# Lo-part stores on GpSimd's queue, and a reordered head of the out-projection, in a two-layer RWKV-7 / sparse-attention trunk

## The chip, the core and the metric

The kernel runs on one core of a Trainium2 chip, in one launch. The time is the device time of one execution, in microseconds (us); a kernel's time is the median of its runs. A core has five engines with a queue each, worked off in order: TensorE (PE; its weight loads are shown apart as PEld), VectorE (DVE), ScalarE (ACT), GpSimd (POOL) and SyncE (SP), which here only issues DMAs. Engines wait for one another through semaphores.

## The reference

A residual stream of 16 learned meta tokens and 512 tokens, 1024 wide, goes through two layers. All is float32.

```
for i in range(2):                                   # layer
    h = h + 0.5 * swiglu(rms_norm(h, g[0]), w_in[i, 0], w_out[i, 0])      # 1024 -> 2 x 2816 -> 1024
    hn = rms_norm(h, g[1])
    if i == 0: h = h + rwkv7_time_mix(hn, ...)
    else:      h = h + dsa_attention(hn, ...)
    h = h + 0.5 * swiglu(rms_norm(h, g[2]), w_in[i, 1], w_out[i, 1])
return h[:, 16:]

def rwkv7_time_mix(h, mix, w_r, w_k, w_v, w_o, ..., g1, g2, ...):
    xx = shift_by_one_token(h) - h
    xr, xw, xk, xv, xa, xg = h + xx * mix[0..5]       # six mixed inputs
    r, k, v = xr @ w_r, xk @ w_k, xv @ w_v
    decay, a = low-rank functions of xw, xa
    g = sigmoid(xg @ g1) @ g2                         # the gate, rank 160
    y = recurrence over the tokens, 16 heads of 64
    return ((group_norm(y) * lnx_g + lnx_b + bonus) * g) @ w_o            # the out-projection
```

## The kernel before

Activations lie transposed: channels on the 128 partitions in eight tiles (`d` or `m`, 0 to 7), tokens along the free axis. The tokens are cut into two ranges, A (272, the meta tokens among them) and B (256), and each stage is done for one range at a time. Every float32 product is made of three TensorE passes: weights and activations are split in a rounded part `hi` and the rest `lo`, and `mm3` adds hi x hi, hi x lo and lo x hi. An input tile with its two parts is a "pair" (`p`, 14 buffers); `acc` are four PSUM banks for long sums, `bg` three for short ones, `ry` one.

Weights come from HBM as units of 128 x 1024 (512 KB), in the order of use. For each, SP loads `wraw` (4 buffers), ScalarE rounds it to `whi` and VectorE subtracts to get `wlo` (4 buffers each). `Weights.take` hands TensorE a block and sees to it that the units up to `ahead` (two further on) are split. A part of the `wlo` is kept: "save" and "keep" units are written to HBM (`lo`) by a DMA on SP's queue, behind the subtraction, and a later "again" unit reads it back in place of the subtraction. There are 32 such stores: 26 in about the first 200 us, six (units 4 to 9 of the out-projection's weights) in the out-projection of A.

The order of the work is that of the program text; generators are interleaved by hand (`joined`, `early`, counting steps) and by a planner that estimates times (`run`). In layer 0 the second half of the first FFN for B (`f00b`) is followed by `joined`: the out-projection of A, with the first steps of the projection of B (`proj`) inside it. Later the FFN `f01a` of A is followed by the out-projection of B.

The FFN ends with residuals: `finish(m)` adds the sum of tile `m` to `h` (VectorE), squares the result for the next norm (ScalarE) and adds the square to `ss` (VectorE). A `Lag` holds such small work back for some ticks, and `lag.flush()` issues what is left at the end.

`outproj` begins with `gate(m)`: five matmuls give the gate of tile `m` in a `bg` bank; VectorE multiplies it with the recurrence's output (`tb`, for A in two pieces, 256 and 16 wide), ScalarE rounds the product and VectorE subtracts, which makes the pair that the out-projection reads. Three gates go first; then, for `d` = 0 to 7, gate `d + 3` and the three products of tile `d` into three `acc` banks; then, for `m` = 3 to 7, eight products and the residual (`end`). The statistics of the next norm for B are asked for at a given step (`early(..., at=9)`), on TensorE four matmuls of `ones` with `ss` and `last`, and on VectorE a Newton iteration on `nst`.

`proj` begins with mixes: `mix(i, d)` makes one of the 6 x 8 mixed inputs: VectorE writes the normed tile (`ynat`), the token difference (`bu`) and the mixed tile (`tb`), ScalarE rounds, and VectorE subtracts (`p`) when the next mix has been issued. For B the first three of them are done within the out-projection of A, one each at the steps 27, 31 and 35 of its 51; the first weights, those of the key, then go over the eight inputs in four banks at a time.

Of the kernel before, what the change touches and what calls it, by code (L numbers as in the profile page):

```python
# [202 lines left out]
class Weights:  # L203


    def __init__(self, nc, pool, dram, wall, plan, raw_bufs, bufs, ahead):
        units, order = plan
        self.nc, self.pool, self.dram, self.wall = nc, pool, dram, wall
        self.units, self.kind, self.key = [units[u] for u, _, _ in order], [o[1] for o in order], [o[2] for o in order]
        self.raw_bufs, self.bufs, self.ahead = raw_bufs, bufs, ahead  # L210
        self.flat = [(i, p) for i, unit in enumerate(self.units) if self.kind[i] != "save" for p in unit]
        start = 128 * np.concatenate([[0], np.cumsum([unit_width(u) for u in units])])
        self.start = [start[u] for u, _, _ in order]
        self.pos = self.nraw = self.nhi = self.nlo = self.nback = 0
        self.raw, self.hi, self.lo, self.saved = {}, {}, {}, {}

    def load(self):

# [20 lines left out]
    def split(self, last):  # L239

        while self.nlo <= min(last, len(self.units) - 1):
            u = self.nlo
            self.round(u)
            self.back(u)
            r = self.raw.pop(u)
            w = r.shape[1]
            if self.kind[u] != "again":
                lo = self.pool.tile([128, 1024], F32R, name="wlo", bufs=self.bufs)
                self.nc.vector.tensor_sub(lo[:, :w], r, self.hi[u][:, :w].bitcast(F32))
                self.lo[u] = lo  # L250
            if self.kind[u] in ("save", "keep"):
                d = self.saved[self.key[u]] = self.dram.tile([128, 1024], F32, name=f"lo{self.key[u]}")
                self.nc.sync.dma_start(d, lo.bitcast(F32))
            self.nlo += 1

    def back(self, last):
# [14 lines left out]
    def take(self, piece):  # L271
        u, (p, at) = self.flat[self.pos]
        assert p == piece, (self.pos, p, piece)
        n = self.ahead + ("save" in self.kind[u + 1:u + 4])
        self.split(u + n)
        self.back(u + 3)
        if at >= 512:
            self.round(u + n + 1)
        self.pos += 1
        s = slice(at, at + piece[3] - piece[2])  # L280
        return self.hi[u][:, s], self.lo[u][:, s]
# [253 lines left out]
def trunk(ctx, tc, wall, plan, h0, vec, cstd, gqk, out, stop=None, gap=0.0, share=400.0, slack=200.0, fulls={}):  # L535
# [176 lines left out]


    def ffn(l, j, r, X, HID, nxt=None, done=None, groups=(0, 4), norm=None, xdone=None, tanh=False,
            part=None, side=False):


        win, wout = f"win{l}{j}", f"wout{l}{j}"
# [34 lines left out]
        for g in range(*groups):  # L753
# [74 lines left out]
            for m in range(3, DT):  # L828
# [7 lines left out]
                    if f == f0 + 1:  # L836
                        next(steps, None)
                lag.later(1, lambda m=m, p=p: finish(m, p, last))
        lag.flush()


    chains = []
# [105 lines left out]
    def proj(R, norm, pairs, core, ahead, park=None):  # L948
# [76 lines left out]
        if pad:  # L1025
            for t in (R.BKV[:, :, 8, 1:3, pad:], R.P[:, :, 8, 1 + pad:], R.a[:, :, n:288]):
                nc.gpsimd.memset(t, 0.0)
        for _ in range(4 if park else 3):
            mixes(1)
            yield  # L1030

# [453 lines left out]
        e = shi[32:64, 1, :n]  # L1485
        nc.vector.tensor_sub(e, R.sg[32:64, 1, :n], e.bitcast(F32))

    def outproj(R, pairs, nxt, last=None):

        r = R.r  # L1490
        n = R.n - R.pad
        shi, slo = (t for _, t in R.gates)
        xs, slot = {}, {}

        def gate(m):
            p = bbank()
# [9 lines left out]
                nc.vector.scalar_tensor_tensor(t[:, 256:n], y[:, 8, :R.pad], col(LNB + m), p[:, 256:n],  # L1506
                                               op0=OP.add, op1=OP.mult)
            slot[m] = pairs.take()
            xs[m] = [slot[m][1][:, j, :n] for j in range(2)]
            split(*xs[m], t[:, :n])  # L1510

        def end(m, p):
            residual(m, r, p[:, :n], 1.0)
            nxt.add(m, r)

        for m in range(3):
            gate(m)
            yield
        ps = [bank() for _ in range(3)]
        for d in range(DT):  # L1520
            if d + 3 < DT:
                gate(d + 3)
            if d + 3 == DT - 1:
                for t in R.gates:
                    pairs.give(t)
                if last:
                    last()
# [21 lines left out]
                norms[0].add(i // 4 - 4, B)  # L1549
            yield c  # L1550

    def ffn_stage(l, j, r, nxt, name, X=None, steps=None, other=None, xdone=None, HID=None, part=None):
        norm = norms[3 * l + 2 * j]
        if other:
            X = Rows(pairs, r)
# [12 lines left out]
            X.give()  # L1568
            return xdone if xdone else iter(())

        main = ffn(l, j, r, X, HID, nxt, norm=norm if other else None, xdone=free, part=part)
        run(early(first(main), norm, B, at=64, X=lambda: other, start=180, every=30) if other else main, name)
        HID.give()

# [4 lines left out]
    def joined():  # L1579

        main = proj(RB, norms[1], pairs, core, stepsA)
        for i, c in enumerate(early(outproj(RA, pairs, norms[2]), norms[1], B, at=9, apart=4)):
            if i in (27, 31, 35):
                assert B in norms[1].rstd
                next(main)
            yield c
        yield from early(main, norms[2], A, at=100, apart=16)

    mid, right = ExitStack(), ExitStack()
    pairs = Pairs(right.enter_context(tile_pool("pairs", side="right")), 14)  # L1590
    core = mid.enter_context(tile_pool("core"))
# [32 lines left out]
            yield c  # L1624

    run(prefix(proj(RA, norms[1], pairs, core, stepsB, HB)), "pA")
    ffn_stage(0, 0, B, norms[1], "f00b", XB, stepsB, xdone=gates(RA), HID=HB, part="rest")
    drain()
    core_work(RB, core, S)
    run(joined(), "pB")  # L1630
    ffn_stage(0, 1, A, norms[3], "f01a", XA, stepsA, xdone=gates(RB))
    drain()
    XS = {}
    xa = []
# [15 lines left out]
        for _ in steps:  # L1650
            pass

    run(early(first_x(outproj(RB, pairs, norms[2], after)), norms[3], A, at=9, apart=4))
    right.close()
    xq = xa[0]

# [458 lines left out]
```

## Time and profile before

| | before |
|---|---|
| time, median of 3 runs (lowest, highest) | 2252.68 us (2248.6, 2252.9) |
| the profiled execution: its own time, its span | 2253.37 us, 2251.6 us |
| mean granted TensorE clock | 0.996 |
| moved by DMA | 405.66 MB, mean 180 GB/s |
| time of a 512 KB load of `wraw` / store of `lo` / read of `lo`, issue to landing | 3.5 / 4.2 / 4.4 us |

The profile is one execution. Times are us from the span's start. In rows of the trace, an operation stands as engine, line, operation, output<-input, shape; "[0.50 <-ACT p L387]" says that the engine stood idle 0.50 us before it and that ScalarE's work on `p` ended that. In lists of waits, the numbers are the total, the number and the longest. Nearly every instruction has the line of one helper, so that the names of the tiles tell them apart.

### The profile page before, as it was taken

The page shows a single profiled execution, that of the slowest core. Times are in us where ns is not written, and L with a number is a line of the kernel's source. Part 1 is how long each engine was busy: PE and PEld are TensorE (multiplying, and loading weights), DVE is VectorE, ACT ScalarE, POOL GpSimd, SP SyncE. Part 2 cuts the span into 40 slices and gives each one's busy share as a digit, 9 for nine tenths or more (in the row PEclk, how much of TensorE's full clock was granted, in tenths as well). Part 3 has the DMA queues.
Part 4 walks back from the last instruction along what each step waited for, and adds up shares of the span by engine and source line. Part 5 has one row for each costly group of instructions (what it writes and reads, how often), then busy time and mean ns, then how long its engine had stood idle before and what let it go on. Part 6 is the DMA issues. An engine that isn't in the chain of part 4 may idle for free.

```text
span 2251.6 us, 49304 instructions
## 1 busy us (share of the span) xinstructions
PE 2209.3 (98%) x20028; PEld 2147.2 (95%) x20028; DVE 1643.9 (73%) x3281; ACT 1261.6 (56%) x2189; POOL 70.5 (3%) x122
## 2 busy tenths in 40 slices
PE   8999999999999999999999999999999999999999
PEld 8999999999899999999999999899998989989999
DVE  7777787846878883676656659887667988867665
ACT  6555784486478447654445445556545645555443
POOL 0000002011000110000000000000000000000000
PEclk9999999999999999999999999999999999999999
DMA  8788766622585562365555655553455543435654
GB/s 283 276 295 280 277 217 236 197 68 88 198 296 177 161 195 79 103 221 185 178 172 167 194 164 169 164 172 129 144 180 162 172 151 106 149 104 179 191 184 140
DMA packets 115188, 405.66 MB, mean 180 GB/s; under 512 B 12993, under 2 KB 17169, under 8 KB 114961
## 3 DMA queue, kind: packets, MB, share of 16 engines
q1 hardware_dynamic: 112592, 397.07, 53.0%
q0 software_dynamic: 2368, 5.44, 0.9%
q8 instruction: 157, 2.57, 0.5%
q14 instruction: 71, 0.57, 0.1%
HBM read 380.88 MB, written 21.05 MB: 179 GB/s over the span
## 4 chain that ended last, share of the span: by engine, by line
PE 82%; DVE 10%; ACT 4%; issue 2%; DMA 1%; SPq 0%; ACTq 0%; DVEq 0%
PE acc L387 70%; PE bg L387 9%; PE ry L387 4%; DVE wlo L387 3%; DMA wraw<-wall 1%; ACT whi L387 1%; DVE tb L387 1%; DVE ynat L387 1%; DVE p L387 1%; DVE rel L387 1%; DVE h L387 1%; DVE m L387 0%; ACT pr L387 0%; DVE AR L387 0%; ACT p L387 0%
## 5 line engine op out<-in xcount | busy, mean ns | idle before, releaser
L387 ACT ACTIVATE whi<-wraw 128x1024 fp32r<-128x1024 f32 (+2 forms) x674 | 705.6, 1052 | 412.0 <-PE acc L387 244.3
L387 DVE TENSOR_TENSOR wlo<-wraw,whi 128x1024 fp32r<-128x1024 f32 (+3 forms) x628 | 766.1, 1223 | 187.8 <-ACT whi L387 173.4
L387 PE MATMUL acc<-p,whi 128*128 128x272 f32 (+1 forms) x4112 | 790.0, 291 | 14.6 <-ACT whi L387 6.7
L387 PEld LDWEIGHTS acc<-p,whi 128*128 128x128 f32 x4112 | 644.9, 190 | 23.7 <-DVE p L387 7.2
L387 PE MATMUL acc<-p,wlo 128*128 128x272 f32 (+1 forms) x2056 | 590.4, 287 | 0.2 <-DVE wlo L387 0.2
L387 PEld LDWEIGHTS acc<-p,wlo 128*128 128x128 f32 x2056 | 389.8, 190 | 0.6 <-DVE wlo L387 0.6
L387 PE MATMUL acc<-xa_hi,whi 128*128 128x256 f32 (+1 forms) x1072 | 306.6, 286 | 0.0
L387 PE MATMUL acc<-xa_hi,wlo 128*128 128x256 f32 (+1 forms) x1072 | 304.3, 284 | 1.0 <-DVE wlo L387 1.0
L387 PE MATMUL acc<-xa_lo,whi 128*128 128x256 f32 (+1 forms) x1072 | 303.7, 283 | 0.0
L387 PE MATMUL acc<-hid_hi,whi 128*128 128x256 f32 (+1 forms) x880 | 253.0, 288 | 1.3 <-DVE ta L387 1.0
L387 PE MATMUL acc<-hid_lo,whi 128*128 128x256 f32 (+1 forms) x880 | 250.1, 284 | 4.3 <-DVE hid_lo L387 4.3
L387 PE MATMUL acc<-hid_hi,wlo 128*128 128x256 f32 (+1 forms) x880 | 249.9, 284 | 0.0
L387 PE MATMUL acc<-xb_hi,whi 128*128 128x256 f32 x744 | 211.3, 284 | 0.0
L387 PE MATMUL acc<-xb_hi,wlo 128*128 128x256 f32 x744 | 208.7, 280 | 0.0
L387 PE MATMUL acc<-xb_lo,whi 128*128 128x256 f32 x744 | 208.6, 280 | 0.0
L387 PEld LDWEIGHTS acc<-xa_hi,whi 128*128 128x128 f32 x1072 | 202.8, 189 | 1.6 <-issue 1.5
L387 PEld LDWEIGHTS acc<-xa_hi,wlo 128*128 128x128 f32 x1072 | 202.7, 189 | 1.4 <-DVE wlo L387 1.4
L387 PEld LDWEIGHTS acc<-xa_lo,whi 128*128 128x128 f32 x1072 | 203.0, 189 | 0.0
L387 PEld LDWEIGHTS acc<-hid_lo,whi 128*128 128x128 f32 x880 | 168.1, 191 | 5.2 <-DVE hid_lo L387 5.2
L387 PEld LDWEIGHTS acc<-hid_hi,whi 128*128 128x128 f32 x880 | 166.9, 190 | 3.9 <-issue 1.9
L387 DVE SCALAR_TENSOR_TENSOR h<-acc,h 128x256 f32<-128x256 f32 (+1 forms) x288 | 117.3, 425 | 71.5 <-PE acc L387 71.2
L387 PEld LDWEIGHTS acc<-hid_hi,wlo 128*128 128x128 f32 x880 | 167.2, 190 | 0.0
(309 smaller groups left out, 3156.9 us busy)
## 6 DMA issues: line engine op xcount, KB each, us to landing
wraw<-wall SPq DMA_DIRECT2D x659, 512.0 KB, 3.5
wlo<-lo SPq DMA_DIRECT2D x46, 512.0 KB, 4.4
lo<-wlo SPq DMA_DIRECT2D x32, 512.0 KB, 4.2
wraw<-wall SPq DMA_DIRECT2D x10, 438.0 KB, 3.3
out<-h SPq DMA_DIRECT2D x8, 256.0 KB, 2.3
h<-h SPq DMA_DIRECT2D x2, 512.0 KB, 8.1
L<-gm POOLq DMA_DIRECT2D x16, 64.0 KB, 2.4
ynat<-L POOLq DMA_DIRECT2D x2, 512.0 KB, 4.9
```

Of the source, the lines that this page charges most:

```text
L387: r = f(*args, **kw)
```

## The change

It has five parts. The stores of `lo` are issued by GpSimd in place of SP. `gate` no longer subtracts at once: it leaves the subtraction to the next gate (`lower`), so that VectorE does gate `m + 1`'s multiplication between. The FFN ahead of an out-projection does not flush its lag: the out-projection gets it as `tail`, and ticks or flushes it after each of its first three gates. While these gates are issued, `W.hold` keeps `take` from splitting units ahead. And in `joined` the statistics for B are asked for at step 5 in place of 9, and five mixes of B are done ahead, at the steps 19, 24, 29, 34 and 39.

```diff
@@ -213,6 +213,7 @@
         self.start = [start[u] for u, _, _ in order]
         self.pos = self.nraw = self.nhi = self.nlo = self.nback = 0
         self.raw, self.hi, self.lo, self.saved = {}, {}, {}, {}
+        self.hold = False
 
     def load(self):
 
@@ -250,7 +251,7 @@
                 self.lo[u] = lo
             if self.kind[u] in ("save", "keep"):
                 d = self.saved[self.key[u]] = self.dram.tile([128, 1024], F32, name=f"lo{self.key[u]}")
-                self.nc.sync.dma_start(d, lo.bitcast(F32))
+                self.nc.gpsimd.dma_start(d, lo.bitcast(F32))
             self.nlo += 1
 
     def back(self, last):
@@ -271,7 +272,7 @@
     def take(self, piece):
         u, (p, at) = self.flat[self.pos]
         assert p == piece, (self.pos, p, piece)
-        n = self.ahead + ("save" in self.kind[u + 1:u + 4])
+        n = 0 if self.hold else self.ahead + ("save" in self.kind[u + 1:u + 4])
         self.split(u + n)
         self.back(u + 3)
         if at >= 512:
@@ -712,7 +713,7 @@
 
 
     def ffn(l, j, r, X, HID, nxt=None, done=None, groups=(0, 4), norm=None, xdone=None, tanh=False,
-            part=None, side=False):
+            part=None, side=False, tail=None):
 
 
         win, wout = f"win{l}{j}", f"wout{l}{j}"
@@ -836,7 +837,10 @@
                     if f == f0 + 1:
                         next(steps, None)
                 lag.later(1, lambda m=m, p=p: finish(m, p, last))
-        lag.flush()
+        if tail is None:
+            lag.flush()
+        else:
+            tail.append(lag)
 
 
     chains = []
@@ -1025,7 +1029,7 @@
         if pad:
             for t in (R.BKV[:, :, 8, 1:3, pad:], R.P[:, :, 8, 1 + pad:], R.a[:, :, n:288]):
                 nc.gpsimd.memset(t, 0.0)
-        for _ in range(4 if park else 3):
+        for _ in range(4 if park else 5):
             mixes(1)
             yield
 
@@ -1485,12 +1489,12 @@
         e = shi[32:64, 1, :n]
         nc.vector.tensor_sub(e, R.sg[32:64, 1, :n], e.bitcast(F32))
 
-    def outproj(R, pairs, nxt, last=None):
+    def outproj(R, pairs, nxt, tail, last=None):
 
         r = R.r
         n = R.n - R.pad
         shi, slo = (t for _, t in R.gates)
-        xs, slot = {}, {}
+        xs, slot, late = {}, {}, []
 
         def gate(m):
             p = bbank()
@@ -1506,20 +1510,34 @@
                 nc.vector.scalar_tensor_tensor(t[:, 256:n], y[:, 8, :R.pad], col(LNB + m), p[:, 256:n],
                                                op0=OP.add, op1=OP.mult)
             slot[m] = pairs.take()
-            xs[m] = [slot[m][1][:, j, :n] for j in range(2)]
-            split(*xs[m], t[:, :n])
+            hi, lo = xs[m] = [slot[m][1][:, j, :n] for j in range(2)]
+            lower()
+            nc.scalar.activation(hi, t[:, :n], AF.Copy)
+            late.append(lambda: nc.vector.tensor_sub(lo, t[:, :n], hi.bitcast(F32)))
+
+        def lower():
+            while late:
+                late.pop()()
 
         def end(m, p):
             residual(m, r, p[:, :n], 1.0)
             nxt.add(m, r)
 
+        W.hold = True
         for m in range(3):
             gate(m)
+            if m < 2:
+                tail.tick()
+            else:
+                tail.flush()
             yield
+        W.hold = False
         ps = [bank() for _ in range(3)]
         for d in range(DT):
             if d + 3 < DT:
                 gate(d + 3)
+            else:
+                lower()
             if d + 3 == DT - 1:
                 for t in R.gates:
                     pairs.give(t)
@@ -1549,7 +1567,7 @@
                 norms[0].add(i // 4 - 4, B)
             yield c
 
-    def ffn_stage(l, j, r, nxt, name, X=None, steps=None, other=None, xdone=None, HID=None, part=None):
+    def ffn_stage(l, j, r, nxt, name, X=None, steps=None, other=None, xdone=None, HID=None, part=None, tail=None):
         norm = norms[3 * l + 2 * j]
         if other:
             X = Rows(pairs, r)
@@ -1568,7 +1586,8 @@
             X.give()
             return xdone if xdone else iter(())
 
-        main = ffn(l, j, r, X, HID, nxt, norm=norm if other else None, xdone=free, part=part)
+        main = ffn(l, j, r, X, HID, nxt, norm=norm if other else None, xdone=free, part=part,
+                   tail=tail)
         run(early(first(main), norm, B, at=64, X=lambda: other, start=180, every=30) if other else main, name)
         HID.give()
 
@@ -1579,13 +1598,14 @@
     def joined():
 
         main = proj(RB, norms[1], pairs, core, stepsA)
-        for i, c in enumerate(early(outproj(RA, pairs, norms[2]), norms[1], B, at=9, apart=4)):
-            if i in (27, 31, 35):
+        for i, c in enumerate(early(outproj(RA, pairs, norms[2], *tails[0]), norms[1], B, at=5, apart=4)):
+            if i in (19, 24, 29, 34, 39):
                 assert B in norms[1].rstd
                 next(main)
             yield c
         yield from early(main, norms[2], A, at=100, apart=16)
 
+    tails = [], []
     mid, right = ExitStack(), ExitStack()
     pairs = Pairs(right.enter_context(tile_pool("pairs", side="right")), 14)
     core = mid.enter_context(tile_pool("core"))
@@ -1624,11 +1644,11 @@
             yield c
 
     run(prefix(proj(RA, norms[1], pairs, core, stepsB, HB)), "pA")
-    ffn_stage(0, 0, B, norms[1], "f00b", XB, stepsB, xdone=gates(RA), HID=HB, part="rest")
+    ffn_stage(0, 0, B, norms[1], "f00b", XB, stepsB, xdone=gates(RA), HID=HB, part="rest", tail=tails[0])
     drain()
     core_work(RB, core, S)
     run(joined(), "pB")
-    ffn_stage(0, 1, A, norms[3], "f01a", XA, stepsA, xdone=gates(RB))
+    ffn_stage(0, 1, A, norms[3], "f01a", XA, stepsA, xdone=gates(RB), tail=tails[1])
     drain()
     XS = {}
     xa = []
@@ -1650,7 +1670,7 @@
         for _ in steps:
             pass
 
-    run(early(first_x(outproj(RB, pairs, norms[2], after)), norms[3], A, at=9, apart=4))
+    run(early(first_x(outproj(RB, pairs, norms[2], *tails[1], after)), norms[3], A, at=9, apart=4))
     right.close()
     xq = xa[0]
 
```

TensorE's queue keeps its order but for those statistics and the spreading of their result, which come earlier. VectorE's first gates of A, before: `h_71<-acc` are the FFN's residuals, `ss` sums of squares, `tb` and `p` a gate's product and its subtraction, `wlo` a weight subtraction.

```order
L387 SCALAR_TENSOR_TENSOR h_71<-acc_7961,h_71 128x256
L387 TENSOR_TENSOR ss_7901<-ss_7901,tb_7994 128x256
L387 SCALAR_TENSOR_TENSOR h_71<-acc_7982,h_71 128x256
L387 TENSOR_TENSOR ss_7901<-ss_7901,tb_8004 128x256
L387 TENSOR_TENSOR wlo_8011<-wraw_7834,whi_7985 128x1024
L387 SCALAR_TENSOR_TENSOR tb_8018<-AR_4001,vecs_83,bg_8010 128x256
L387 SCALAR_TENSOR_TENSOR tb_8018<-AR_4001,vecs_83,bg_8010 128x16
L387 TENSOR_TENSOR p2_8021<-tb_8018,p2_8021 128x272
L387 SCALAR_TENSOR_TENSOR tb_8030<-AR_4001,vecs_83,bg_8024 128x256
L387 SCALAR_TENSOR_TENSOR tb_8030<-AR_4001,vecs_83,bg_8024 128x16
L387 TENSOR_TENSOR p9_8033<-tb_8030,p9_8033 128x272
```

The same place of VectorE's queue now:

```order
L388 SCALAR_TENSOR_TENSOR h_71<-acc_7961,h_71 128x256
L388 SCALAR_TENSOR_TENSOR tb_8009<-AR_4001,vecs_83,bg_8003 128x256
L388 SCALAR_TENSOR_TENSOR tb_8009<-AR_4001,vecs_83,bg_8003 128x16
L388 TENSOR_TENSOR ss_7901<-ss_7901,tb_7994 128x256
L388 SCALAR_TENSOR_TENSOR h_71<-acc_7982,h_71 128x256
L388 SCALAR_TENSOR_TENSOR tb_8024<-AR_4001,vecs_83,bg_8018 128x256
L388 SCALAR_TENSOR_TENSOR tb_8024<-AR_4001,vecs_83,bg_8018 128x16
L388 TENSOR_TENSOR p2_8012<-tb_8009,p2_8012 128x272
L388 TENSOR_TENSOR ss_7901<-ss_7901,tb_8015 128x256
L388 SCALAR_TENSOR_TENSOR tb_8039<-AR_4001,vecs_83,bg_8033 128x256
L388 SCALAR_TENSOR_TENSOR tb_8039<-AR_4001,vecs_83,bg_8033 128x16
L388 TENSOR_TENSOR p9_8027<-tb_8024,p9_8027 128x272
```

The first product stands ahead of the last residual, the first weight subtraction (`wlo_8011` before) behind all of this, and a gate's subtraction behind the next gate's product.

VectorE's queue at the first mixes of B, before (residuals `h_71<-acc` are those of the out-projection of A; the residual in the first row is that of `m` = 5):

```order
L387 SCALAR_TENSOR_TENSOR h_71<-acc_8326,h_71 128x272
L387 TENSOR_TENSOR ss_8237<-ss_8237,tb_8385 128x272
L387 SCALAR_TENSOR_TENSOR ynat_8336<-h_71,vecs_83,rstd_8283 128x256
L387 TENSOR_TENSOR bu_8340<-ynat_8336 128x256
L387 SCALAR_TENSOR_TENSOR tb_8396<-bu_8340,vecs_83,ynat_8336 128x256
L387 TENSOR_TENSOR p3_8352<-tb_8350,p3_8352 128x256
L387 SCALAR_TENSOR_TENSOR h_71<-acc_8388,h_71 128x272
L387 TENSOR_TENSOR ss_8237<-ss_8237,tb_8427 128x272
L387 SCALAR_TENSOR_TENSOR h_71<-acc_8430,h_71 128x272
```

The same place of VectorE's queue now, from the fourth mix on:

```order
L388 TENSOR_TENSOR p7_8337<-tb_8335,p7_8337 128x256
L388 SCALAR_TENSOR_TENSOR h_71<-acc_8349,h_71 128x272
L388 TENSOR_TENSOR ss_8242<-ss_8242,tb_8399 128x272
L388 SCALAR_TENSOR_TENSOR ynat_8298<-h_71,vecs_83,rstd_8239 128x256
L388 TENSOR_TENSOR bu_8302<-ynat_8298 128x256
L388 SCALAR_TENSOR_TENSOR tb_8426<-bu_8302,vecs_83,ynat_8298 128x256
L388 TENSOR_TENSOR p0_8369<-tb_8367,p0_8369 128x256
L388 SCALAR_TENSOR_TENSOR h_71<-acc_8402,h_71 128x272
L388 TENSOR_TENSOR ss_8242<-ss_8242,tb_8441 128x272
L388 SCALAR_TENSOR_TENSOR h_71<-acc_8444,h_71 128x272
```

The last three residuals had two, three and three mixes ahead of them; now they have four, five and five, and three subtractions of mixes are done before the last two residuals in place of one.

GpSimd's queue in the out-projection of A, which held only the clears (`MEMSET`) there, now, with the six stores (`lo18` to `lo23`):

```order
L388 MEMSET p4_7907 128x272
L388 DMA lo18_8105<-wlo_8103 128x1024
L388 DMA lo19_8167<-wlo_8165 128x1024
L388 DMA lo20_8206<-wlo_8204 128x1024
L388 DMA lo21_8255<-wlo_8253 128x1024
L388 DMA lo22_8292<-wlo_8290 128x1024
L388 MEMSET gm_8304 128x64
L388 DMA lo23_8352<-wlo_8350 128x1024
L388 MEMSET rs_9294 128x288
```

The clear of `gm` (a column of B's decays) stands behind five stores, each of which waits for its subtraction; on SP's queue the loads follow one another without them.

## The prediction

> **What bounds the kernel now.** I read the page's busy shares first, then TensorE's waits over the stretch that the change touches, then that stretch engine by engine in order of time.
>
> ```profile
> PE 2209.3 (98%) x20028; PEld 2147.2 (95%) x20028; DVE 1643.9 (73%) x3281; ACT 1261.6 (56%) x2189; POOL 70.5 (3%) x122
> ```
>
> TensorE is busy 98% of 2251.6 us, so a change that leaves its matmuls alone can win only its pauses (some 42 us) and the time that it runs at a lower clock. Two lists of what TensorE waited for follow: 540 to 660 us, which holds the out-projection of the first token range (A), and 975 to 1030 us, which holds that of the second (B).
>
> ```profile
> PE acc L387 <- DVE p L387: 3.7, 3, 1.8
> PE bg L387 <- DVE tb L387: 1.8, 1, 1.8
> PE acc L387 <- DVE h L387: 0.4, 1, 0.4
> ...
> PE bg L387 <- DVE tb L387: 0.6, 1, 0.6
> ```
>
> All are waits for VectorE. At A they fall at 587.8 us (fourth gate), 621.4 us (first mixed input of the next projection) and shortly after; one of the 3.7 us stands earlier, in the FFN. The stage table (us, TensorE busy, weight loads, VectorE, ScalarE, POOL, clock, DMA) shows that they cost more than their length:
>
> ```profile
> 585.00:590.00 5.00, 3.18 (x20) 2.91 (x19) 3.87 (x11) 1.96 (x5) 0.00 (x0) 0.88 0.44 151
> 590.00:595.00 5.00, 5.00 (x33) 5.00 (x33) 3.65 (x10) 2.64 (x5) 0.00 (x0) 0.78 0.00 0
> ...
> 620.00:625.00 5.00, 2.67 (x13) 2.17 (x14) 4.30 (x12) 2.98 (x7) 0.00 (x0) 0.79 1.02 415
> 625.00:630.00 5.00, 5.00 (x25) 5.00 (x26) 4.79 (x13) 3.01 (x5) 0.00 (x0) 0.53 1.02 399
> ```
>
> After either pause the granted clock falls; the four rows lose 5 x (0.12 + 0.22 + 0.21 + 0.47) = 5.1 us to it.
>
> Under those pauses VectorE is never free for long. Its queue at the gates of A:
>
> ```profile
> 584.30 0.42 DVE L387 SCALAR_TENSOR_TENSOR h<-acc,h 128x256 f32<-128x256 f32 x1
> 584.64 0.41 DVE L387 TENSOR_TENSOR ss<-ss,tb 128x256 f32<-128x256 f32 x1
> ...
> 585.87 1.22 DVE L387 TENSOR_TENSOR wlo<-wraw,whi 128x1024 fp32r<-128x1024 f32 x1
> 587.00 0.62 DVE L387 SCALAR_TENSOR_TENSOR tb<-AR,vecs,bg 128x256 f32<-128x256 f32 x2
> 588.12 0.44 DVE L387 TENSOR_TENSOR p<-tb,p 128x272 fp32r<-128x272 f32 x1 [0.50 <-ACT p L387]
> 588.48 0.61 DVE L387 SCALAR_TENSOR_TENSOR tb<-AR,vecs,bg 128x256 f32<-128x256 f32 x2
> 589.59 0.44 DVE L387 TENSOR_TENSOR p<-tb,p 128x272 fp32r<-128x272 f32 x1 [0.50 <-ACT p L387]
> ...
> 601.83 0.44 DVE L387 TENSOR_TENSOR p<-tb,p 128x272 fp32r<-128x272 f32 x1 [0.50 <-ACT p L387]
> 602.78 1.23 DVE L387 TENSOR_TENSOR wlo<-wraw,whi 128x1024 fp32r<-128x1024 f32 x1 [0.51 <-ACT whi L387]
> 603.92 0.15 DVE L387 TENSOR_SCALAR nst<-bg 128x2 f32<-128x2 f32 x1
> ...
> 606.16 0.78 DVE L387 SCALAR_TENSOR_TENSOR h<-acc,h 128x272 f32<-128x272 f32 x2
> 607.50 0.44 DVE L387 TENSOR_TENSOR ss<-ss,tb 128x272 f32<-128x272 f32 x1 [0.56 <-ACT tb L387]
> ```
>
> Each of the eight gates makes VectorE stand 0.50 us for ScalarE's rounding before it can subtract. From start to start, a weight subtraction takes 1.13, a residual or a sum of squares 0.34, a gate's multiply pair with its subtraction 0.90 (1.47 less 0.50, and less the overlap of back-to-back work), the norm's statistics 2.24 (603.92 to 606.16). Then the mixes, two of TensorE's groups of three, and ScalarE's first copy of a finished key group:
>
> ```profile
> 620.95 0.41 DVE L387 TENSOR_TENSOR p<-tb,p 128x256 fp32r<-128x256 f32 x1
> 621.29 0.43 DVE L387 SCALAR_TENSOR_TENSOR h<-acc,h 128x272 f32<-128x272 f32 x1
> 622.27 0.44 DVE L387 TENSOR_TENSOR ss<-ss,tb 128x272 f32<-128x272 f32 x1 [0.56 <-ACT tb L387]
> ...
> 622.98 0.48 DVE L387 SCALAR_TENSOR_TENSOR ynat<-h,vecs,rstd 128x256 f32<-128x256 f32 x1
> ...
> 624.36 0.42 DVE L387 TENSOR_TENSOR p<-tb,p 128x256 fp32r<-128x256 f32 x1
> 624.69 0.48 DVE L387 SCALAR_TENSOR_TENSOR ynat<-h,vecs,rstd 128x256 f32<-128x256 f32 x1
> ...
> 630.20 0.40 PE L387 MATMUL acc<-p,whi 128*128 128x256 f32 x2
> ...
> 630.56 0.40 PE L387 MATMUL acc<-p,whi 128*128 128x256 f32 x2
> ...
> 631.20 0.42 DVE L387 TENSOR_TENSOR p<-tb,p 128x256 fp32r<-128x256 f32 x1
> ...
> 635.07 0.39 ACT L387 ACTIVATE BKV<-acc 128x256 f32<-128x256 f32 x1 [1.53 <-PE acc L387]
> ```
>
> A mix of the first kind with its subtraction costs 1.71 us (622.98 to 624.69); the eight inputs are served at that pace, the sixth at 631.20. TensorE needs 0.36 us for three matmuls, 1.43 for an input's twelve. So from 584 to 632 us the path is VectorE's queue, and a place in that queue is worth something only by the bubbles that it closes.
>
> **The change part by part.** *Gates in front of the last residuals, subtraction one gate late, weight work held.* No instruction is added. Laid end to end from 584.30 in the new order: two residuals and two sums 1.36, eight gates 7.2, five weight subtractions 5.65 (as many as before up to that point), the statistics 2.24, now between the fifth and sixth subtraction of a gate: 16.5, so A's first output residual comes at 600.8 instead of 606.16, 5.4 earlier. Of it 8 x 0.50 + 0.51 = 4.5 are named waits. The fourth gate's bank is free when its third has issued, so the 1.8 us pause goes. What is late next: at 0.125 a matmul a gate takes TensorE 0.62 and an input's nine 1.13, so it is ready for the sixth gate's input at 595.7, which now stands behind the statistics and comes at 597.1; a pause of some 1.4, and one of 0.8 at the seventh, which cost nothing as long as VectorE sets the end. The hold makes the third weight unit's subtraction 2 us later (587.9), read by TensorE at 589.7.
>
> *Five mixes from the 20th step instead of three from the 28th.* Same work, moved ahead of three of the residuals that follow. From 600.8 in the new order, a residual and its sum 1.3 (0.99 of it to the sum, with the 0.56 wait for ScalarE), weight work 1.13, mixes 1.38 to 1.71: the first input is ready at 614.6, before TensorE wants it (617: the last gate's matmuls end at 601.4, and the 120 that follow take 0.125 each), the third at 619.4, the sixth at 626.0 against 631.20. Late next: the key group needs four banks, and the third and fourth are given back by the last two residuals, now behind the fifth mix, at 619.9 and 621.2. TensorE then pauses about 3 us around 618 to 621, and then runs 1.43 us per input behind the mixes: the first key copy comes at 629.5 against 635.07. I take 5.6 us for A; bounds: 2.2, if two more stretches at half clock (6.8 us, a loss of 3.4) follow that pause, and 10.2 less B's 0.6, if every pause named (1.8 + 1.8 + 0.4 + 0.5 + 0.6 = 5.1) and all 5.1 us of low clock went. Nearest is VectorE's queue, which leads both ends.
>
> *The same gates at B* have 0.6 us to win; the first input's subtraction comes some 0.25 after TensorE could use it: 0.4 (0 to 0.6).
>
> *Stores by POOL.* 32 issues move from SP, 26 of them in the first 200 us, six at A.
>
> ```profile
> lo<-wlo SPq DMA_DIRECT2D x32, 512.0 KB, 4.2
> ynat<-L POOLq DMA_DIRECT2D x2, 512.0 KB, 4.9
> DVE wlo L387 <- DMA lo<-wlo: 11.6, 6, 2.6
> 20.00:200.00 180.00, 179.35 (x1430) 178.71 (x1430) 135.08 (x226) 96.15 (x135) 0.00 (x0) 1.00 0.80 278
> L387 POOL DMA_DIRECT2D L<-gm x18: 584/648/730, 367.3 to 779.5; - x18
> ```
>
> The loads behind a store on SP's queue wait for the same subtraction anyway, since it frees the raw buffer that they fill; what a load gains is the issue of 0.33 us and a shorter line. TensorE pauses 0.65 us in those 180 us, so at most 0.7 is to be won. Worst, each store lands 0.7 later (4.9 against 4.2) and all of it reaches TensorE: 32 x 0.7 = 22. But VectorE already stands 11.6 us behind store landings without a pause of TensorE, being two weight units ahead (24 matmuls each, at 179.35 / 1430 = 0.125: 6.0 us): I take 0. POOL pays 32 x 0.65 us; it is 97% idle, and what stands behind its stores at A, a clear of a decay column, is first read by the scan at 666:
>
> ```profile
> 666.20 0.71 DVE L387 TENSOR_TENSOR_SCAN gm<-reset,gm 128x264 f32<-128x264 f32 x1 [3.39 <-ACT gm L387]
> ```
>
> Sum: 5.6 + 0.4 + 0 = 6.0 off the profiled execution, 2253.4 to 2247.4. That execution was 0.7 above the median of the three runs shown, so against 2252.7 I predict 2246.7.
>
> *A rule beside a row.* The clock fell after a pause of 1.8 us with matmuls on both sides. The Trainium skill's page "TensorE: Matmul & The Clock Gate" (What's actually happening) lets the clock drop after at least one idle window of about 3.4 us. By that rule no pause here would cost clock, and removing all of them would give 5.1; the rows show the 5.1 of lost clock as well, and the rows decide.
>
> **The rivals.** *New pauses eat it.* For it: VectorE's queue is no shorter, and residuals now stand behind mixes. Gain 2.2 + 0.4 at the low bound, up to 4: 2248.7 to 2250.1. Against: the bubbles closed (4.5) are real waits in the rows.
>
> *All pauses and all low clock go.* 10.2 off: 2242.5. Against: the queue laid end to end closes only 5.4.
>
> *POOL's stores come too late: slower.* If a store issued by POOL starts much later than SP's did while VectorE is busy, the weight buffer stays taken, VectorE waits, then TensorE. It decides once a store lands over 6 us later than now; at 0.5 us reaching TensorE for each of 26 stores, 13 us: 2259.7. Against: POOL issued 18 transfers in 584 to 730 ns each in stretches where VectorE was busy. The Trainium skill's page "SBUF — State Buffer" (SBUF: two separate sides) says that VectorE's two-port modes lock GpSimd out of the port through which it writes its descriptors; those issues show none of it.
>
> **How the numbers follow.** My case, 4 to 7 us: 0.55; new pauses, 1 to 4: 0.25; everything goes: 0.13; slower: 0.07. Within 0.2% (4.5 us) is about what a measurement here cannot tell from no change. Faster by more: nine tenths of the first and the third, 0.63; same: the rest of the first and the second, 0.32; slower: 0.05, as some of that case stays within 0.2%. The range reaches from the third case's edge, 2243.5, to the weak end of the second, 2251.5.
>
> **What would show it.** Right: no 0.50 waits at A's gates, first residual near 601, first key copy near 629.5, a pause of TensorE for a residual near 619, no pause over 1 us at the fourth gate. Wrong: half clock still after 619 for two stretches, the first key copy after 632, or TensorE pausing for weights before 200 us.

## The result, and the profile after

The changed kernel takes 2269.78 us (median of 6 runs, 2267.28 to 2271.33) against 2251.55 (2248.6 to 2252.9) of the kernel before on the same chip: a ratio of 1.0084, with a 95% interval of 1.0073 to 1.0094. It is slower by 0.84%, 18 us. The profiled executions differ by less, 2267.28 against 2253.37, 13.9 us; the sums below are made against those.

From the page of the changed kernel, the busy shares and the stores of `lo` (size, median us from issue to landing):

```profile
PE 2208.7 (97%) x20028; PEld 2145.2 (95%) x20028; DVE 1642.4 (72%) x3281; ACT 1260.4 (56%) x2189; POOL 86.4 (4%) x154
...
lo<-wlo POOLq DMA_DIRECT2D x32, 512.0 KB, 6.3
```

A store now lands 6.3 us after its issue, where it was 4.2. The stage table of the changed kernel shows where that matters (columns as in the prediction), and the same first two stretches of before stand behind it:

```profile
20.00:98.00 78.00, 77.70 (x625) 77.47 (x624) 61.06 (x123) 42.33 (x67) 6.38 (x12) 1.00 0.80 263
98.00:235.00 137.00, 122.12 (x932) 119.33 (x931) 89.29 (x134) 63.83 (x83) 7.72 (x19) 0.98 0.76 251
165.00:170.00 5.00, 2.26 (x10) 2.26 (x11) 4.25 (x6) 1.38 (x2) 0.00 (x0) 0.75 0.39 125
170.00:175.00 5.00, 5.00 (x38) 5.00 (x38) 3.99 (x7) 3.39 (x4) 0.53 (x1) 0.90 0.92 259
230.00:235.00 5.00, 2.72 (x16) 2.72 (x17) 4.01 (x12) 2.23 (x4) 0.00 (x0) 0.74 0.44 133
235.00:240.00 5.00, 5.00 (x29) 5.00 (x28) 2.41 (x9) 1.06 (x1) 0.00 (x0) 0.58 0.68 239
```

```profile
20.00:98.00 78.00, 77.75 (x625) 77.53 (x625) 60.47 (x122) 42.59 (x69) 0.00 (x0) 1.00 0.74 263
98.00:235.00 137.00, 134.58 (x1071) 133.19 (x1069) 105.56 (x175) 74.64 (x103) 0.00 (x0) 1.00 0.86 293
```

Up to 98 us the two are alike, although 12 stores fall there. Between 98 and 235 us, where a save unit comes after every three units that TensorE uses, TensorE's busy time falls from 134.58 to 122.12 us. Twice it falls far enough for the clock to be halved: 5 x (0.25 + 0.10 + 0.26 + 0.42) = 5.2 us more. A pause of TensorE at the end of the FFN ahead of the out-projection, ahead of all that the change reorders there, serves as a mark; in the timeline of before, and then of after:

```profile
572.17 0.39 PE L387 MATMUL acc<-p,whi 128*128 128x256 f32 x1 [1.45 <-DVE p L387]
```

```profile
591.69 0.39 PE L388 MATMUL acc<-p,whi 128*128 128x256 f32 x1 [1.45 <-DVE p L388]
```

At the mark the kernel is 19.5 us late. VectorE's waits between 98 and 225 us of the changed kernel (total, times, longest) name the cause; TensorE's between 98 and 235 us stand behind them:

```profile
DVE wlo L388 <- DMA lo<-wlo: 18.0, 5, 4.1
DVE wlo L388 <- issue: 15.8, 5, 5.1
...
PE acc L388 <- DVE wlo L388: 5.5, 4, 1.7
PE acc L388 <- DVE ta L388: 4.2, 1, 4.2
PE bg L388 <- DVE ss L388: 2.6, 1, 2.6
```

"issue" stands for a wait whose end the profile does not name. All five of that line end 0.08 us behind the landing of a store (at 144.94, for one, behind a landing at 144.86), so they are the same wait. TensorE waits for `wlo` itself, and for `ta` and `ss`, which stand in VectorE's queue behind a subtraction that is held; before, it had none of these three waits here. A piece of VectorE's and then POOL's timeline shows one turn:

```profile
128.07 1.23 DVE L388 TENSOR_TENSOR wlo<-wraw,whi 128x1024 fp32r<-128x1024 f32 x1 [0.78 <-ACT whi L388]
...
133.95 1.23 DVE L388 TENSOR_TENSOR wlo<-wraw,whi 128x1024 fp32r<-128x1024 f32 x1 [3.96 <-DMA lo<-wlo]
...
135.45 1.22 DVE L388 TENSOR_TENSOR wlo<-wraw,whi 128x1024 fp32r<-128x1024 f32 x1
136.98 1.22 DVE L388 TENSOR_TENSOR wlo<-wraw,whi 128x1024 fp32r<-128x1024 f32 x1 [0.31 <-ACT whi L388]
...
127.24 0.53 POOL L388 DMA_DIRECT2D lo<-wlo  x1 [9.94 <-DVE wlo L388]
138.50 0.53 POOL L388 DMA_DIRECT2D lo<-wlo  x1 [10.73 <-DVE wlo L388]
```

POOL issues each store 0.3 us behind its subtraction, so POOL is not late. The second subtraction after a save here needs the save's buffer (the other three of the four `wlo` buffers hold the unit that TensorE reads and the two ahead), and stands until the store has landed. The held one is followed by one more and by that of the next save, whose store is then issued: a closed loop of 138.50 - 127.24 = 11.3 us, of which 6.7 is the landing (with 0.2 from it to the subtraction) and 4.6 are three subtractions. TensorE uses up three units in 72 x 0.125 = 9.0 us. With a landing of 4.2 the loop would be some 9.0 us (an estimate: 4.2, the same 0.2 and 4.6), as long as TensorE's 9.0; with 6.3 it is over it. Not each turn is so long: of the twelve from the store at 98.3 us to that at 221.5, the second subtraction is held in seven, of 10.5 to 12.4 us, and a later one or none in five, of 8.4 to 9.6. On the average they take 10.3 us, where before, from 98.8 to 207.7, they took 9.1: 12 x 1.2 = 14.4 us. That is the pauses; the half clock, 5.2, is the rest of the 19.5, as near as these sums go.

Then the out-projection of A in the changed kernel, by engine: VectorE's first output residual, the first mixed input's subtraction, the sixth's, the last residual; TensorE's pauses for residuals; ScalarE's first copy of a key group; and the clock.

```profile
621.09 0.78 DVE L388 SCALAR_TENSOR_TENSOR h<-acc,h 128x272 f32<-128x272 f32 x2
...
634.92 0.42 DVE L388 TENSOR_TENSOR p<-tb,p 128x256 fp32r<-128x256 f32 x1
...
641.38 0.43 DVE L388 SCALAR_TENSOR_TENSOR h<-acc,h 128x272 f32<-128x272 f32 x1
...
646.53 0.42 DVE L388 TENSOR_TENSOR p<-tb,p 128x256 fp32r<-128x256 f32 x1
...
640.52 0.50 PE L388 MATMUL acc<-p,whi 128*128 128x256 f32 x2 [2.44 <-DVE h L388]
641.87 0.49 PE L388 MATMUL acc<-p,whi 128*128 128x256 f32 x1 [0.73 <-DVE h L388]
...
651.94 0.39 ACT L388 ACTIVATE BKV<-acc 128x256 f32<-128x256 f32 x1 [1.75 <-PE acc L388]
...
640.00:645.00 5.00, 3.75 (x18) 3.55 (x19) 4.30 (x12) 3.46 (x7) 0.00 (x0) 0.70 1.03 402
```

From the mark to the first key copy it takes 60.25 us, before 635.07 - 572.17 = 62.90: a gain of 2.65. The out-projection of B gains 0.9 (the delay goes from 16.9 to 16.0), and after a later pause the clock is not halved where it was before, worth some 2 (last section). 19.5 - 2.65 - 0.9 - 2 is the 13.9.

### The profile page after: what moved, and what is told of

It reads as the page before. It is cut to its first block, busy times and chain, and to the rows that moved or that the text cites. A ratio compares the mean times of both kernels' runs of the same rounds, so it can differ in the third digit from the quotient of the medians.

```text
span 2265.5 us, 49343 instructions
## 1 busy us (share of the span) xinstructions
PE 2208.7 (97%) x20028; PEld 2145.2 (95%) x20028; DVE 1642.4 (72%) x3281; ACT 1260.4 (56%) x2189; POOL 86.4 (4%) x154
## 4 chain that ended last, share of the span: by engine, by line
PE 59%; DVE 6%; ACT 2%; issue 1%; DVEq 0%; ACTq 0%
PE acc L388 51%; PE bg L388 6%; PE ry L388 2%; DVE wlo L388 2%; DVE rel L388 1%; DVE m L388 1%; ACT whi L388 1%; ACT pr L388 0%; DVE sc L388 0%; DVE tb L388 0%; DVE h L388 0%; DVE pr L388 0%; DVE hid_lo L388 0%; DVE qst L388 0%; DVE xb_lo L388 0%
```

## The experiments

Ratios are to the kernel before, run beside each kernel on the same chip; intervals are 95%. The kernel before took 2249.37 us beside the first four experiments here (stores undone, alone, by kind, own buffer), 2250.85 beside the stores by ScalarE and the three on mixes and statistics, and 2249.91 beside the other three. Edits are shown against the changed kernel unless it says otherwise.

### The stores, undone and alone

```diff
-                self.nc.gpsimd.dma_start(d, lo.bitcast(F32))
+                self.nc.sync.dma_start(d, lo.bitcast(F32))
```

> The changed kernel with the stores issued by SP again; what is left of the change is the out-projection. Buffer theory (a store issued by POOL lands 6.6 us after its subtraction in place of 4.3, and the second subtraction after it needs its buffer) and traffic theory (the second queue slows the loads of raw weights) both put the whole loss on the stores: then the two out-projections keep what the trace of the changed kernel shows for them, 2.5 + 0.9 us, so about 2248 against 2251.6, and TensorE pauses less than 1 us between 98 and 220 us. Out-projection theory (the reordered head costs time): 2252 or more.

2248.31 us, ratio 0.9990 (0.9982 to 0.9999). The opposite edit in the kernel before:

> The kernel before with nothing changed but the issuer of the 32 stores, POOL in place of SP. Buffer and traffic theory: the loss of the stretch between 98 and 255 us alone, 14.3 us of pauses and 5.1 us of half clock, so about 2271 (2266 to 2274, by how the half-clock stretches fall). Out-projection theory: 2251 to 2254.

2270.87, ratio 1.0094 (1.0078 to 1.0109). The stores alone make the loss, and all of it; without them the change is faster by 0.1%. That the first of these two took the 2248 us that I had named is luck: the gain that I had named with it was 3.4 us, and it is 1.1.

### Which stores

```diff
-                self.nc.gpsimd.dma_start(d, lo.bitcast(F32))
+                (self.nc.sync if self.kind[u] == "save" else self.nc.gpsimd).dma_start(d, lo.bitcast(F32))
```

> The changed kernel with the 14 save stores (90 to 222 us, one for every three units that TensorE uses) issued by SP, and the 18 keep stores (12 before 90 us, six in the out-projection of A) by POOL. Buffer theory: the keep stores cost nothing, since those before 90 us have two units of 3.0 us and the freed buffers of units that were used behind them: 2248 to 2250, as with all stores by SP. Traffic theory: 18 of 32 stores keep their share of the loss, so 2258 or more, with pauses of TensorE before 90 us or in the out-projection of A.

2248.62, ratio 0.9995 (0.9986 to 1.0004). The 18 keep stores by POOL land in 6.4 us and cost nothing that can be measured; the 14 save stores make the loss.

### A buffer that nobody waits for

```diff
-                lo = self.pool.tile([128, 1024], F32R, name="wlo", bufs=self.bufs)
+                if self.kind[u] == "save":
+                    lo = self.own.tile([128, 1024], F32R, name="prod", bufs=1)
+                else:
+                    lo = self.pool.tile([128, 1024], F32R, name="wlo", bufs=self.bufs)
...
+    W.own = core
```

> The changed kernel, all stores by POOL, but the lo part of a save unit goes to a buffer of its own (the one named prod, unused until the first recurrence), so that no weight buffer waits for a store of that kind; the next save is over 9 us later. Buffer theory: the stores still land over 6 us after issue, no subtraction into wlo waits for them, TensorE's pauses between 98 and 220 us go, 2248 to 2250. Traffic theory: the same packets on the same two queues, so the loss stays: 2267 or more.

2248.42, ratio 0.9990 (0.9981 to 0.9999): the whole loss is gone, with all 32 stores still on POOL's queue. Between 98 and 225 us, VectorE's and TensorE's waits and the store:

```profile
DVE prod L391 <- DMA lo<-prod: 2.7, 2, 1.6
...
PE acc L391 <- ACT p L391: 0.5, 1, 0.5
PE acc L391 <- DVE h L391: 0.2, 1, 0.2
...
lo<-prod POOLq DMA_DIRECT2D x13, 512.0 KB, 6.5
```

The landing is as late as ever, 6.5 us, and no subtraction into `wlo` waits for it. So it is the buffer, and not the traffic: the same packets ran on the same two queues.

### Why a store lands late: whose queue

```diff
-                self.nc.gpsimd.dma_start(d, lo.bitcast(F32))
+                self.nc.scalar.dma_start(d, lo.bitcast(F32))
```

> The changed kernel with the 32 stores issued by ScalarE, whose queue is a hardware one as SP's is. If the late landing belongs to POOL's software queue, a store lands 4 to 5 us after issue, and no loop of late stores forms between 98 and 220 us; what is new is that ScalarE's next rounding stands behind a store that waits for a subtraction of 1.2 us. I expect 2249 to 2254. If any second queue beside SP's lands late, landing is over 6 us and the time is near 2268.

2273.83, ratio 1.0101 (1.0087 to 1.0115), a miss for the theory that POOL's software queue is slow. Between 98 and 225 us, VectorE's wait and the store:

```profile
DVE wlo L388 <- DMA lo<-wlo: 26.5, 10, 4.1
...
lo<-wlo ACTq DMA_DIRECT2D x12, 512.0 KB, 7.0
```

A hardware queue of its own is no better. What both have in common is that SP's loads run beside the store. So the queues were swapped; the loads went to POOL, the stores to SP:

```diff
-        self.nc.sync.dma_start(r[:, :n], self.wall[...
+        (self.nc.gpsimd if "save" in self.kind[u:] else self.nc.sync).dma_start(r[:, :n], self.wall[...
...
-                self.nc.gpsimd.dma_start(d, lo.bitcast(F32))
+                self.nc.sync.dma_start(d, lo.bitcast(F32))
```

> The changed kernel with queues swapped: the stores by SP, and the loads of raw weights by POOL as far as the last save unit (then by SP again). A store by ScalarE's hardware queue landed as late as one by POOL. Sharing theory (on one queue a store is served ahead of the loads issued after it; on a queue of its own it shares the 16 DMA engines with them): stores land in about 6 us here too, though SP issues them, the subtractions wait for them by 4 us, and TensorE pauses for wlo between 98 and 220 us; 2262 to 2275, more if the loads themselves come late. Issuer theory (SP is simply the quick issuer): stores land in 4.3 us or less and no subtraction waits over 2.6 us for one.

2262.51, ratio 1.0050 (1.0035 to 1.0066). About 6 us of it is another thing: the first loads come later, and TensorE starts at 12.2 us in place of 6.2. VectorE's waits between 98 and 225 us, the store there, and all the stores by 230 us (shortest, median, longest landing):

```profile
DVE wlo L388 <- DMA lo<-wlo: 22.0, 9, 3.6
...
lo<-wlo SPq DMA_DIRECT2D x13, 512.0 KB, 5.4
...
DMA to landing us min/median/max: 2.6/5.0/6.2
```

Issued by SP, with SP's queue to itself, a store takes 2.6 to 2.7 us when POOL's queue moves next to nothing meanwhile (packets of 6 to 28 KB overlap it), and 5.2 to 6.2 when it moves 1.0 to 1.4 MB. So sharing makes a store late, whoever issues it. At like traffic the issuers differ little: beside 1.3 to 1.4 MB, SP's stores here took 5.9 and 6.2 us, and POOL's in the changed kernel 5.7 to 6.4. Whether they differ with the engines to themselves is not shown, as only SP's stores had that. On the loads' own queue a store stands only behind the loads issued before it. On another queue it shares the 16 engines with those that come after it too: in the changed kernel's save stretch 1.4 MB of loads moved while a store was under way (median of 13), and with the stores on SP again 0.9. Both the start and the transfer are longer: in the changed kernel the first packet of a store moved 2.7 us after its issue and the last 3.3 us later (medians of 13), where SP's with next to nothing beside them needed 0.8 and 1.5. The Trainium skill's page "DMA: Bandwidth & Descriptors" (Queues, rings and completion order) says that each engine takes turns, packet by packet, between the queues that have work for it; these traces agree, as in those 3.3 us 0.63 MB of loads moved beside the store's 0.52.

### The out-projection: five mixes or three

What the change gains at A varies with the clock. From the mark to the first key copy, the kernels with all stores by SP, with the save stores by SP and with the buffer of its own, whose out-projection is that of the changed kernel, take 61.43, 62.34 and 60.15 us, with 6.8, 10.2 and 3.4 us at half clock in that stretch; the changed kernel had 3.4. So the 2.65 above is one execution's; these are 0.6 to 2.75.

From here on the stores are issued by SP, and edits are shown against that kernel.

```diff
-        for _ in range(4 if park else 5):
+        for _ in range(4 if park else 3):
...
-            if i in (19, 24, 29, 34, 39):
+            if i in (27, 31, 35):
```

> Stores by SP, gates and lag as changed, statistics at step 5, but three mixes at the steps 27, 31 and 35 as before. Residual theory (with five mixes TensorE waits for the last two residuals of the out-projection, which stand behind them, and from there on it sets the end itself): the last residual comes two mixes, 3.4 us, earlier, TensorE's pauses of 2.4 and 0.7 us before the key group shrink under 1 us, and VectorE's mixes set the end: eighth input subtracted as late as with five, the first key copy some 1.5 to 2 us earlier, about 2246.5. Queue theory (VectorE's queue sets the end in either case): no difference to five mixes, 2248.3. Theory of the five mixes as the gain: 2250 or more.

2245.92, ratio 0.9978 (0.9968 to 0.9987), 0.12% better than with five (0.9990, 0.9982 to 0.9999), though the intervals still touch. So the opposite edit was made too: five mixes and the early statistics in the kernel before, without the rest.

> The kernel before, stores by SP, with five mixes at the steps 19, 24, 29, 34, 39 and the statistics at step 5, and nothing of the gates, the lag or the hold. Residual theory: gates and first residual stay where they were before, the last residual stands behind two more mixes, TensorE waits for it until about 627 and needs some 11 us from there to the first key copy: 638 in place of 635, so 2 to 3 us slower than before, 2252. Queue theory: VectorE's work is the same, so no difference to before, 2249.4.

2254.08, ratio 1.0016 (1.0007 to 1.0025): five mixes, with the early statistics, cost 3 us there. TensorE's last pause ahead of the key group there, and the first key copy:

```profile
626.28 0.80 PE L387 MATMUL acc<-p,whi 128*128 128x256 f32 x2 [0.73 <-DVE h L387]
...
636.28 0.39 ACT L387 ACTIVATE BKV<-acc 128x256 f32<-128x256 f32 x1 [1.68 <-PE acc L387]
```

TensorE gets its last bank at 626.28 and needs 10.0 us from there, where the residual theory had about 627 and some 11: the mechanism is right.

### The statistics, and the parts of the gates

With three mixes, and the statistics back at step 9:

```diff
-        for i, c in enumerate(early(outproj(RA, pairs, norms[2], *tails[0]), norms[1], B, at=5, apart=4)):
+        for i, c in enumerate(early(outproj(RA, pairs, norms[2], *tails[0]), norms[1], B, at=9, apart=4)):
```

> As with three mixes, but the statistics at step 9 as before. If the pauses of 1.1 and 0.6 us at the sixth and seventh gate's input (behind the statistics) cost nothing, as the prediction put it, because VectorE sets the end: they go, and the first key copy stays within 0.5 us of the kernel with three mixes and the statistics at step 5. If TensorE sets it: 1 to 1.7 us earlier.

2245.38, ratio 0.9972 (0.9963 to 0.9981), the fastest kernel here, 0.28% faster than before and by the two ratios some 25 us faster than the change. From the kernel with the statistics at step 5 it cannot be told apart by time. In its trace the mark, the last residual, TensorE's last long pause, VectorE's subtraction of the sixth input and the first key copy:

```profile
570.98 0.39 PE L388 MATMUL acc<-p,whi 128*128 128x256 f32 x1 [1.45 <-DVE p L388]
...
617.17 0.43 DVE L388 SCALAR_TENSOR_TENSOR h<-acc,h 128x272 f32<-128x272 f32 x1
619.37 0.39 PE L388 MATMUL acc<-p,whi 128*128 128x256 f32 x1 [0.91 <-DVE p L388]
...
625.75 0.42 DVE L388 TENSOR_TENSOR p<-tb,p 128x256 fp32r<-128x256 f32 x1
...
628.55 0.38 ACT L388 ACTIVATE BKV<-acc 128x256 f32<-128x256 f32 x1 [0.47 <-PE acc L388]
```

57.57 us from the mark to the key copy, 5.3 less than before, and no stretch at half clock between them. The last residual no longer stops TensorE; it waits for mixes. With the statistics at step 5 it was 59.69, 3.2 less than before: the two are 2.1 apart, where I had expected 0.5 at the most. That execution ran at half clock for 6.83 us from 0.7 us behind the mark on, and its first gate was multiplied 14.6 us behind the mark in place of 12.6, which accounts for the difference. From the kernel with step 9, the lag and the hold were taken out:

```diff
-        W.hold = True
         for m in range(3):
             gate(m)
-            if m < 2:
-                tail.tick()
-            else:
-                tail.flush()
             yield
-        W.hold = False
...
-        if tail is None:
-            lag.flush()
-        else:
+        lag.flush()
+        if tail is not None:
             tail.append(lag)
```

> Of the best so far (stores by SP, three mixes, statistics at step 9) the FFN flushes its lag as before and weights are not held back; of the change only the late subtraction of the gates is left. Bubble theory (the gain is the eight stands of 0.50 us of VectorE, which this closes): within 1 us of the best, 2245 to 2246.5, with a pause of TensorE at the fourth gate that costs little. Order theory (the gain comes from gates ahead of the last residuals): 2248 or more.

2245.91, ratio 0.9983 (0.9975 to 0.9992). And, with lag and hold kept, the late subtraction was taken out:

```diff
             late.append(lambda: nc.vector.tensor_sub(lo, t[:, :n], hi.bitcast(F32)))
+            lower()
```

> Of the best so far (stores by SP, three mixes, statistics at step 9) each gate subtracts at once again, so VectorE stands 0.50 us for ScalarE's rounding at each of the eight; lag and hold stay. Bubble theory: the first key copy 3 to 4 us later than in the best, 2248.5 to 2249.5. Order theory: within 1 us of the best.

2252.32, ratio 1.0008 (0.9999 to 1.0017). The gain of the out-projection is the late subtraction's: without it there is none. From the mark to VectorE's first output residual it is 33.99 us before, 33.86 without the late subtraction, 31.59 without lag and hold, and 29.71 with all of them. The time is over the 2249.5 that I had put as the most: in the trace A takes 4.7 us more from the mark to the key copy than with the late subtraction, with 6.83 us at half clock in it, and I had left out B, which takes 2.0 more. A row of each, the fourth gate's pause without lag and hold, and one of eight stands of VectorE without the late subtraction:

```profile
586.92 0.49 PE L388 MATMUL bg<-p,whi 128*128 128x272 f32 x2 [1.81 <-DVE tb L388]
```

```profile
583.91 0.44 DVE L388 TENSOR_TENSOR p<-tb,p 128x272 fp32r<-128x272 f32 x1 [0.50 <-ACT p L388]
```

Lag and hold remove a pause of 1.8 us, behind which 3.41 us ran at half clock. What that is worth in time stays open: the intervals with and without them overlap (0.9963 to 0.9981, and 0.9975 to 0.9992), and they were taken out together, so that neither is shown alone.

## Why the prediction was wrong, step by step

**Stores by POOL: wrong, and the whole of the loss.** I took 0, on the argument that VectorE already stood 11.6 us behind store landings without a pause of TensorE, being 6 us ahead. That compared one late store with the runway. But the lateness repeats: the store, the buffer, the three subtractions and the next store are a loop, and a loop is held against TensorE's time for as many units. That margin was next to nothing a turn, not 6 us once. The pauses that I set down as the mark of an error, TensorE waiting for weights before 200 us, came. The rival was there, with the right mechanism (buffer, VectorE, TensorE) and 2259.7 us, but its point of decision, "over 6 us later than now", was wrong by the same step: 2.1 us later was enough. So was its reason against: POOL's issues are indeed short, 0.53 us, and that says nothing of the landing. And the landing, which I had 0.7 us later at the worst and which was 2.1 later, was a median of two, 4.9: in the trace of before one of these took 3.7 us with 0.1 MB of loads beside it, the other 6.1 with 1.1 MB. The stores run beside 1.4 MB; the longer was the one to take.

**The gates: right.** First residual predicted 600.8, measured 621.09 - 19.5 = 601.6; first input 614.6, measured 615.4; sixth 626.0, measured 627.0. No stand of 0.50 us at A's gates, no pause over 1 us at the fourth. The experiment without the late subtraction shows that this was the gain.

**Five mixes: the pause was right, its consequence was not.** I named a pause of 3 us for the last two residuals; it was 2.44 + 0.73, at 638 to 642, that is 618.6 to 622.4 by the old times. Then I let the mixes set the end, "1.43 us per input behind the mixes", and put the key copy at 629.5. But when the last bank comes, at 641.87, all but the first matmuls of eight inputs are still to be done, 10.1 us of TensorE to the copy at 651.94, 1.7 of it lost to a stretch at half clock. The mixes would have let it end sooner: the eighth input was subtracted at 648.4, and its twelve matmuls take 1.43, which makes 649.8, or 630.3 by the old times. The path had moved to TensorE behind the last residual, and the end is 632.4. So of the 2.9 us between 629.5 and 632.4, 0.8 are mixes that ended later than I had them, and 2.1 are the step that failed, 1.7 of it as half clock behind the pause. With three mixes, where VectorE does set the end, the best trace has 5.3, nearly the predicted 5.6; it is also the one with no half clock there. The two pauses behind the statistics came as predicted (1.11 and 0.62), and moving the statistics back did not show in the time.

**B: right in kind.** The pause of 0.6 us is gone; 0.9 came of it, above my bound of 0.6. Without lag and hold the pause is back, and 0.7 of the 0.9 is lost, so that at B these two made most of the gain.

**The clock.** Two more stretches of half clock were my low bound for A; there was one, and three (10.2 us, a loss of 5.1) in the save stretch, where I had expected none. Pauses of 2.44 and 0.73 us were enough for it again, as the rows of before had shown.

## What to carry to other kernels

When a transfer holds a buffer that is needed again soon, add up the loop from one such transfer to the next and hold it against the time in which the consumer uses the same units: the slack is the difference of the two, not the run-ahead. A store moved from the loads' queue to one of its own, POOL's or ScalarE's, lost its place in front of the loads that follow; give it a buffer that nobody needs soon, or leave it in line. And when work is moved ahead of the instruction that gives back a bank, count what the waiting engine has still to do after that, at its own pace.

## What the runs showed of the hardware

A 512 KB store issued by SP took 2.6 us with the DMA engines nearly to itself, and 5.2 to 6.2 beside 1.0 to 1.4 MB of loads on another queue. In the save stretch, beside 1.3 to 1.6 MB, it took 5.7 to 7.4 on POOL's queue and 6.2 to 7.6 on ScalarE's hardware queue.

A pause of 3.07 us late in the program is followed by half clock in the kernel before, and not in the changed one. The pause in the timeline and the stage table behind it, before and then after:

```profile
1814.97 0.58 PE L387 MATMUL acc<-hid_lo,whi 128*128 128x256 f32 x1 [3.07 <-DVE hid_lo L387]
...
1815.00:1820.00 5.00, 5.00 (x23) 5.00 (x24) 4.69 (x17) 1.06 (x1) 0.00 (x0) 0.50 0.20 69
```

```profile
1831.31 0.39 PE L388 MATMUL acc<-hid_lo,whi 128*128 128x256 f32 x1 [3.07 <-DVE hid_lo L388]
...
1830.00:1835.00 5.00, 3.34 (x26) 3.14 (x26) 4.76 (x16) 1.44 (x2) 0.00 (x0) 1.00 0.30 105
1835.00:1840.00 5.00, 4.93 (x41) 4.93 (x42) 4.80 (x17) 1.74 (x2) 0.00 (x0) 1.00 0.41 122
```

The half-clock stretches of all these traces last 3.41 or 6.83 us but for the one at the end. The clock is judged on a fixed grid, as the traces show: in each of the 13 the edges of these stretches lie on one grid of 3.413 us, within 0.002 us (the full-clock stretches of the changed kernel between its half-clock ones, of 61.44 and 402.77 us, are 18 and 118 steps of it). So it matters where a pause lies on the grid. Before, this pause left TensorE idle for 2.25 us of one step (1810.75 to 1814.16), and half clock began with the next. In the changed kernel an edge at 1829.83 cut the same pause into 1.58 and 1.49 us, and none followed. In all 13 traces from 20 us on, each full-clock step with over 1.9 us of idle TensorE is followed by half clock, and none with under 1.0; between the two both happened (1.04 was followed by it, 1.89 was not), so idle time within a step is not the whole rule. The same pause can thus cost nothing more, or 1.7 to 3.4 us. That may be a part of the spread between runs of one kernel, and of the 4 us by which the profiled difference of 13.9 and that of the medians, 18.2, disagree; this is not shown.
